# A two-layer hybrid backbone on one core: five sixths of the modulation vectors by GpSimd products and ScalarE row sums in place of TensorE matmuls

## The chip, the cores and the metric

One core of one Trainium2 chip runs the kernel. The time is device microseconds of one execution. TensorE (PE in the rows) multiplies, VectorE (DVE), ScalarE (ACT) and GpSimd (POOL) do the elementwise work, SyncE (SP) issues most of the DMAs. The outputs have to be the reference's to fp32 tolerances.

## What is computed

Two layers over 512 latent tokens and 256 context tokens, 1024 features, fp32. Each layer mixes the tokens in four ways (S5, Hyena long convolution, retention, latent attention) between one input and one output projection, and follows with a gated ConvFFN. Six vectors of 1024 numbers modulate each layer (the shifts, scales and gates of two norms), once from `c` for the latent tokens and once from `c_ctx` for the context:

```python
sc_lat = jax.nn.silu(c)
sc_ctx = jax.nn.silu(c_ctx)
for l in range(DEPTH):
    need_ctx = l < DEPTH - 1
    mod = sc_lat @ ada_w[l] + ada_b[l]
    sh1, sc1, g1, sh2, sc2, g2 = [m[:, None, :] for m in jnp.split(mod, 6, axis=-1)]
    modc = sc_ctx @ ada_w[l] + ada_b[l]
    ...
    h = modulate(rmsnorm(x, norm_g[l, 0]), sh1, sc1)
    y, yc = token_mixing(h, hc, w_in[l], w_out[l], s5_p, hy_p, ret_p, mla_p, need_ctx)
    x = x + g1 * rmsnorm(y, norm_g[l, 1])
    h = modulate(rmsnorm(x, norm_g[l, 2]), sh2, sc2)
    x = x + g2 * rmsnorm(conv_ffn(h, *ffn_p), norm_g[l, 3])
```

So 2 x 6144 columns of `ada_w` are multiplied by two vectors. The modulation is a product of a matrix with a vector or two: 24 MB of weights per layer are read for little arithmetic. In layer 1 the context's shift, scale and gate of the second half are needed by nobody, since the context leaves after layer 0's ConvFFN and layer 1's mixers.

## The kernel before

Features lie on partitions, tokens along the free dimension. Tokens are handled in pieces of 256 (one of the context, two of the latent stream); segment 0 is the context, segment 1 the latent stream. A product of two fp32 matrices is made in three passes of split operands: a weight tile of 128x1024 is loaded (tile `wr`, three buffers), ScalarE casts it to its high part (`wh`, L300), VectorE subtracts that for the low part (`wl`, L301), and TensorE multiplies high by high, high by low and low by high (`dense`, L336). All weight loads, activations, spills and tables go through SP's queue in program order; only a few small DMAs of the S5 and attention chains are issued by GpSimd (`qp`: L946, L947, L1336, L1338). Each engine works through its instructions in one order, which the tile framework's scheduler sets from the program order and priorities.

The modulation vectors come by thirds: `ada(l, b)` makes 2048 columns of layer `l`. It issues 16 loads of 512 KB (L470, tile `ar`, three buffers, which the Hyena chain's tables share), multiplies each with the two silu vectors on TensorE as stationary operand (L475, 64 matmuls a third, 128x32 by 128x512), copies the sum from PSUM (L478), transposes it by four matmuls (L481), and adds the bias. Six thirds: (0,0) at the start; (0,1) and (0,2) by `more`, one piece for each round of `ahead`; (1,0) as a filler of the `drain` that ends layer 0's output projection; (1,1) and (1,2) as a filler of the `drain` that ends layer 0's ConvFFN, and from there in layer 1's `ahead`.

The stages in order: start (norms, (0,0), tables); layer 0's input projection and mixers, woven by `ahead` (a round of every chain that is open for each step of the projection); the output projection, whose last tokens are finished by `live` chains (`finish`: row sum by TensorE, `n_row` by ScalarE L1440, scaling on VectorE, residual addition L1502 on GpSimd and VectorE by halves, squares L1504, modulated tiles H L1467); the ConvFFN (`run(g, W_FF)` at each weight load advances `prep1`, the preparation of layer 1: 62 calls); its last down products with `finish`; then layer 1 likewise. The attention chain (`mla`) splits queries and moves parts of them by DMA on GpSimd's queue (`B_Q`, `B_R`: L1336; `wh`, `wl` from `B_kr`: L1338) before its scores (L1325).

Of the kernel before, what the change touches and what calls it, by code (L numbers as in the profile page):

```python
# [19 lines left out]
L = 2  # L20
D = 1024
# [27 lines left out]
# ---------------------------------------------------------------- host layout  # L49
# [96 lines left out]
def _layout(inp):  # L146
# [5 lines left out]
    o["ada_w"] = _c(inp["ada_w"].reshape(L, KD, 128, 3, 2, 1024).transpose(0, 3, 1, 4, 2, 5))  # L152
# [68 lines left out]
# ---------------------------------------------------------------- the kernel  # L221
@with_exitstack
def tile_kernel(ctx, tc, I, out, dbg=None, upto=None):
# [15 lines left out]
    def tap(name, ap, a, b, k=None):  # L239
        """debug: columns a:b of a tensor (rows k of its tiles)"""  # L240
        if dbg is not None and name in dbg:
            d = dbg[name] if k is None else dbg[name][:, k]
            sp.dma_start(d[..., a:b], ap)
# [45 lines left out]
    # token ranges: segment 0 is the context, segment 1 the latent stream  # L289
# [3 lines left out]
    # ------------------------------------------------------------ helpers  # L293
# [17 lines left out]
    def blk(w, n=128):  # L311
        """tiles k of a loaded weight"""
        return lambda k: (w[0][:, k * n:(k + 1) * n], w[1][:, k * n:(k + 1) * n])

    def passes(W, ks):
        """stationary operand, which part of the moving one (0 high, 1 low), first, last"""
# [7 lines left out]
    def dense(W, X, ks, segs, fine=False, outs=None):  # L324
        """sum over k of W(k)^T X(k, seg, part), per segment into one PSUM bank"""
# [13 lines left out]
    class Job:  # L339
        """a dense product whose parts (256 tokens) may come one by one"""  # L340
# [18 lines left out]
    def ctx_room():  # L359
        """where two jobs share a bank for their context parts"""  # L360
# [11 lines left out]
    def open_jobs(keys, srcs, H, segs):  # L372
        """jobs of the next phase that run while the last tokens of this one are finished"""
# [34 lines left out]
    def rs_rows(p, items, chunks, w=1):  # L408
        """1/rms of columns of 128 tokens: items are ([K, tokens], [K, w]) pairs that add up"""
# [19 lines left out]
    # ------------------------------------------------------------ scratch in DRAM  # L429
# [16 lines left out]
    # ------------------------------------------------------------ adaLN vectors  # L446
# [5 lines left out]
    def ada_setup():  # L452
# [4 lines left out]
        act.activation(c2[:, :, 0:2], craw, AF.Silu)  # L457
        return c2
# [3 lines left out]
    def ada(l, b):  # L462
        """a third of the modulation vectors: 2048 columns"""
        md, der = mods[l]
        ps = sm_ps()
        for k in range(KD):
            raws = []
            for h in range(2):
                raw = new(wp, [128, 1024], "ar", bufs=3)
                qa.dma_start(raw, I["ada_w"][l, b, k, h])  # L470
# [11 lines left out]
        for r in range(2):  # L482
            v = md[:, 16 * b:16 * b + 16, r].rearrange("p (j i) -> p i j", i=4)
            s = pt.rearrange("p (i j x) -> p i j x", i=4, x=32)[:, :, :, r]
            dve.tensor_tensor(v, s, adab[:, l, 16 * b:16 * b + 16].rearrange("p (j i) -> p i j", i=4), ALU.add)
        gb = lambda i: ng[:, l, i].unsqueeze(2).to_broadcast([128, KD, 2])
# [4 lines left out]
        else:  # L491
            dve.scalar_tensor_tensor(der[:, 2], md[:, 32:40], 1.0, gb(2), ALU.add, ALU.mult)
            dve.tensor_tensor(der[:, 3], md[:, 40:48], gb(3), ALU.mult)
        yield

    # ------------------------------------------------------------ S5 parameters
    def reduce_turns(p, lam, n, tag):
        """re*dt, the reduced angle im*dt in turns, from [128, 3, n]"""
# [16 lines left out]
    def sincos(ang, k, out_):  # L515
        """ang[:, 0] holds turns; out_: [128, 2, n], the sine and the cosine"""
# [5 lines left out]
    def s5_prep(l, p):  # L522
# [25 lines left out]
        # a^1: power 1 sits at m = 6 (forward) and m = 1 (backward)  # L548
# [26 lines left out]
        for h in range(2):  # L575
            for d in (1, 0):
# [19 lines left out]
                # state inputs: transposed powers  # L596
# [7 lines left out]
                # state outputs  # L604
# [6 lines left out]
                # within-chunk kernels of two channel groups at a time; each other's are not used  # L611
# [26 lines left out]
        # rotations over chunks  # L638
# [24 lines left out]
    # ------------------------------------------------------------ hyena spectra  # L663
    def planes(al, z, R, room=None):
        """input planes of the classes of frequencies, class by class; z: [128, R/2, 256]; al: room by name"""
# [33 lines left out]
    def hy_spectra(l, p, n, nmx, dst):  # L699
# [33 lines left out]
        for o in range(2):  # L733
# [20 lines left out]
            # columns lie as (direction, channel)  # L754
# [813 lines left out]
    for l in range(L):  # L1568
# [47 lines left out]
        with ExitStack() as base, ExitStack() as esl, ExitStack() as esr:  # L1616
# [5 lines left out]
            if l == 0:  # L1622
# [9 lines left out]
                with mkpool("start", side="right") as px:  # L1632
                    g0 = ada(0, 0)
                    X = []
                    for i, (s, h) in enumerate(subs):
# [4 lines left out]
                        if i == 0:  # L1640
                            c2 = ada_setup()
# [338 lines left out]
```

## Time and profile before

| | |
|---|---|
| runs | 2124.91, 2129.36, 2129.20 us; median 2129.2 |
| profiled execution | span 2130.8 us |
| TensorE busy | 1992.2 us, 93% |
| VectorE, ScalarE, GpSimd busy | 1292.8 (61%), 781.8 (37%), 165.7 us (8%) |
| modulation matmuls (L475) | 384 records, 108.6 us |
| chain of waits | TensorE 77%, VectorE 8%, DMA 7% |

Busy times are sums over the span; stages differ, so a stretch is read by itself. In the tables of stretches each engine's busy time is followed by its instruction count in brackets, then the clock that TensorE was granted (a share of full speed), the busy share of the 16 DMA engines and GB/s. In timelines and the chain a row begins with start and length in us; what stands in square brackets is the engine's idle time before it and what ended it.

### The profile page before, as it was taken

To read this page: it belongs to the slowest core of one execution; us is meant where nothing else is said; L and a number is where in the kernel's file an instruction comes from. 1 tells how busy PE (TensorE), PEld (TensorE's weight loads), DVE (VectorE), ACT (ScalarE), POOL (GpSimd) and SP (SyncE) were. 2 spreads that over 40 slices of the span, in tenths; PEclk is the share of its full clock that TensorE was granted. 3 is DMA by queue.
4 is the path that set the end of the run, shared out by engine and by line. 5 is a ranking of instruction groups with operands and counts; after the bars stand their busy time and mean duration, and the time that the engine had idled before them with its cause. 6 is when DMAs were issued, how large, how long until landed. Compare 5 with 4: busy or idle time off the path is not lost.

```text
span 2130.8 us, 29370 instructions
## 1 busy us (share of the span) xinstructions
PE 1992.2 (93%) x11282; PEld 1558.7 (73%) x11282; DVE 1292.8 (61%) x2594; ACT 781.8 (37%) x1248; POOL 165.7 (8%) x180
## 2 busy tenths in 40 slices
PE   5899999889799999999999999899989989999997
PEld 1676775566687788788888886577766768888885
DVE  5767474786655876674645446367667356555555
ACT  3646322225144534433323234322243435333332
POOL 0121002211001020000000001100013110000000
PEclk7899999889999999999999999999989989999998
DMA  7566556634455434132422215877721314333331
GB/s 254 175 211 225 164 184 185 141 93 125 143 173 167 142 104 138 58 100 66 143 79 60 60 50 175 227 222 234 238 72 51 113 66 148 93 96 99 99 98 41
DMA packets 147092, 282.93 MB, mean 133 GB/s; under 512 B 35605, under 2 KB 78774, under 8 KB 146952
## 3 DMA queue, kind: packets, MB, share of 16 engines
q1 hardware_dynamic: 139016, 272.60, 40.7%
q0 software_dynamic: 3328, 7.13, 1.9%
q10 hardware_dynamic: 4608, 1.31, 0.3%
q8 instruction: 89, 1.46, 0.3%
q14 instruction: 51, 0.42, 0.1%
HBM read 229.07 MB, written 48.99 MB: 130 GB/s over the span
## 4 chain that ended last, share of the span: by engine, by line
PE 77%; DVE 8%; DMA 7%; issue 4%; ACT 2%; POOL 1%; SPq 1%; ACTq 0%; POOLq 0%; DVEq 0%
PE mm L336 44%; PE mm L1830 4%; PE sm L475 4%; DMA ar<-in_ada_w 3%; PE mm L351 2%; PE mm L1938 2%; PE sm L1434 2%; PE mm L1325 1%; PE sm L1380 1%; PE mm L1326 1%; PE mm L332 1%; PE mm L1327 1%; DMA wr<-in_w_v 1%; PE sm L745 1%; PE sm L845 1%
## 5 line engine op out<-in xcount | busy, mean ns | idle before, releaser
L301 DVE TENSOR_TENSOR wl<-wr,wh 128x1024 fp32r<-128x1024 f32 x174 | 212.9, 1225 | 313.8 <-ACT wh L300 309.6
L336 PE MATMUL mm<-H1h,wh 128*128 128x512 f32 x888 | 355.7, 401 | 4.1 <-ACT wh L300 4.0
L336 PE MATMUL mm<-H1h,wl 128*128 128x512 f32 x888 | 355.4, 400 | 0.8 <-DVE wl L301 0.8
L336 PE MATMUL mm<-H1l,wh 128*128 128x512 f32 x888 | 353.2, 398 | 0.0
L300 ACT CAST wh<-wr 128x1024 fp32r<-128x1024 f32 x174 | 182.3, 1050 | 369.2 <-PE mm L336 309.9
L336 PEld LDWEIGHTS mm<-H1h,wh 128*128 128x128 f32 x888 | 169.0, 190 | 52.8 <-ACT wh L300 9.5
L336 PEld LDWEIGHTS mm<-H1l,wh 128*128 128x128 f32 x888 | 168.9, 190 | 42.5 <-issue 5.6
L336 PEld LDWEIGHTS mm<-H1h,wl 128*128 128x128 f32 x888 | 169.0, 190 | 42.3 <-issue 5.0
L336 PE MATMUL mm<-H0h,wh 128*128 128x256 f32 x480 | 136.7, 285 | 5.2 <-DVE st L427 4.2
L336 PE MATMUL mm<-H0l,wh 128*128 128x256 f32 x480 | 138.0, 287 | 0.0
L336 PE MATMUL mm<-H0h,wl 128*128 128x256 f32 x480 | 137.8, 287 | 0.0
L336 PE MATMUL mm<-ff_mh,wh 128*128 128x512 f32 (+1 forms) x432 | 131.1, 357 | 1.0 <-DVE st L427 1.0
L336 PE MATMUL mm<-ff_mh,wl 128*128 128x512 f32 (+1 forms) x432 | 131.3, 357 | 0.0
L336 PE MATMUL mm<-ff_ml,wh 128*128 128x512 f32 (+1 forms) x432 | 130.3, 355 | 0.0
L475 PE MATMUL sm<-ar,ada_c 128*32 128x512 f32 x384 | 108.6, 687 | 16.1 <-DMA ar<-in_ada_w 16.1
L1502 POOL TENSOR_TENSOR x<-x,y 128x512 f32<-128x512 f32 x20 | 28.4, 1427 | 1105.0 <-DVE y L1501 873.1
L1888 DVE TENSOR_TENSOR y<-mm,y 128x512 f32<-128x512 f32 x80 | 53.5, 688 | 81.1 <-PE mm L336 80.9
L336 PEld LDWEIGHTS mm<-H0h,wh 128*128 128x128 f32 x480 | 92.0, 192 | 13.1 <-issue 9.5
L336 PEld LDWEIGHTS mm<-H0h,wl 128*128 128x128 f32 x480 | 91.6, 191 | 7.0 <-issue 6.9
L336 PEld LDWEIGHTS mm<-H0l,wh 128*128 128x128 f32 x480 | 91.5, 191 | 5.6 <-issue 5.3
L425 ACT ACTIVATE st<-mm,c_ffn_v 128x512 f32<-128x512 f32 (+1 forms) x132 | 88.7, 701 | 5.3 <-PE mm L351 5.3
L426 DVE SCALAR_TENSOR_TENSOR st<-mm,c_ffn_v,st 128x511 f32<-128x511 f32 (+1 forms) x132 | 83.0, 654 | 3.7 <-ACT st L425 3.7
(617 smaller groups left out, 4178.0 us busy)
## 6 DMA issues: line engine op xcount, KB each, us to landing
ar<-in_ada_w SPq DMA_DIRECT2D x96, 512.0 KB, 4.3
wr<-in_w_up SPq DMA_DIRECT2D x88, 512.0 KB, 3.6
wr<-in_w_down SPq DMA_DIRECT2D x44, 512.0 KB, 3.6
wr<-in_w_in SPq DMA_DIRECT2D x34, 512.0 KB, 4.8
wr<-in_w_out SPq DMA_DIRECT2D x16, 512.0 KB, 4.4
ar<-in_k_tabl SPq DMA_DIRECT2D x16, 512.0 KB, 3.7
xs_d<-x SPq DMA_DIRECT2D x8, 1024.0 KB, 5.6
pd<-st SPq DMA_DIRECT2D x19, 384.0 KB, 2.7
```

Of the source, the lines that this page charges most:

```text
L300: act.copy(hi, raw)
L301: dve.tensor_tensor(lo, raw, hi.bitcast(F32), ALU.subtract)
L336: pe.matmul(outs[s], w, X(k, s, j), start=f, stop=z)
L351: pe.matmul(self.outs[s][:, h:h + 256], w, X(k, s, j)[:, h:h + 256], start=f, stop=z)
L425: act.activation(u[:, o:o + m], ps, AF.Identity, bias=vw[:, 3:4], scale=vw[:, 1:2])
L426: dve.scalar_tensor_tensor(u[:, o + 1:o + m], ps[:, 0:m - 1], vw[:, 0:1], u[:, o + 1:o + m], ALU.mult, ALU.add)
L475: pe.matmul(ps[q:q + 32], c2[:, k], raws[h][:, j * 512:(j + 1) * 512], start=(k == 0), stop=(k == KD - 1))
L1434: pe.matmul(self.ps[q:q + 32, :256], ones32, sq[:, i], start=(self.k < 4), stop=(self.k >= KD - 4))
L1502: (pool, dve)[k // 2 % 2].tensor_tensor(x[:, ks], x[:, ks], y[:, ks], ALU.add)
L1830: pe.matmul(ps[:, m * 256:(m + 1) * 256], w, C[s][j][:, k, h:h + 256], start=f and not e and m == 0, stop=z and m == 1)
L1888: dve.tensor_tensor(d, ps, d, ALU.add)
L1938: pe.matmul(ps[:, m * 256:(m + 1) * 256], w, mid[k][j][:, tk:tk + 256], start=f, stop=z)
```

## The change

The weights of five thirds are stored transposed: 128 output columns on partitions, 1024 inputs along them, one tile of 512 KB for 128 outputs. `silu(c)` and `silu(c_ctx)` are broadcast over partitions once (two DMAs, two ScalarE activations). For each tile GpSimd multiplies elementwise (L519), and ScalarE copies the product onto itself with a row sum into the modulation vector (L520). The context's product goes to a single buffer `ada_s`, the other overwrites the weights. There are 16 tiles a third; two products each for layer 0's two thirds and for (1,0), one each for (1,1) and (1,2), which leave the context's out: 128 products and 128 row sums, with 80 loads as before. The first third (`ada_first`) stays on TensorE. 320 of the 384 matmul records go, with 5 ScalarE copies and 20 transposes. By the code all of layer 1's thirds run in `prep1`; the two drains lose their filler. A smaller scratch for GpSimd's DMAs makes room for the new tiles.

```diff
     o["c"] = ...
-    o["ada_w"] = _c(inp["ada_w"].reshape(L, KD, 128, 3, 2, 1024).transpose(0, 3, 1, 4, 2, 5))
+    aw = inp["ada_w"]
+    o["ada_w"] = _c(aw[0, :, :2048].reshape(KD, 128, 2, 1024).transpose(0, 2, 1, 3))
+    o["ada_t0"] = _c(aw[0, :, 2048:].T.reshape(32, 128, D))
+    o["ada_t1"] = _c(aw[1].T.reshape(48, 128, D))
+    o["c_row"] = _c(np.stack([inp["c"][0], inp["c_ctx"]]))
...
         act.activation(c2[:, :, 0:2], craw, AF.Silu)
+        for v in range(2):
+            sp.dma_start(cb[v], I["c_row"][v:v + 1].to_broadcast([128, D]))
         return c2
...
+    cb = [new(con, [128, D], f"c_bc{v}") for v in range(2)]
+
+    def ada_first():
...
+    def ada(l, b):
+        md = mods[l][0]
+        nr = 2 if l == 0 or b == 0 else 1
+        for m in range(16 * b, 16 * b + 16):
+            w = new(wp, [128, D], "ar", bufs=3)
+            qa.dma_start(w, I["ada_t0"][m - 16] if l == 0 else I["ada_t1"][m])
+            for r in reversed(range(nr)):
+                t = new(con, [128, D], "ada_s") if r else w
+                pool.tensor_tensor(t, w, cb[r], ALU.mult)
+                act.activation(t, t, AF.Copy, accum_out=md[:, m, r:r + 1])
+            if m % 2:
+                yield
+        for r in range(nr):
+            v = md[:, 16 * b:16 * b + 16, r]
+            dve.tensor_tensor(v, v, adab[:, l, 16 * b:16 * b + 16], ALU.add)
+        ada_gains(l, b, nr)
         yield
...
-                    g0 = ada(0, 0)
+                    g0 = ada_first()
...
                             c2 = ada_setup()
+                    for v in range(2):
+                        act.activation(cb[v], cb[v], AF.Silu)
...
-                ga = ada(1, 0) if l == 0 else iter(())
-                drain(open_jobs([("up", i) for i in range(n)], [fl(I["w_up"][l, i]) for i in range(n)], H, lambda k: segs), ga)
+                drain(open_jobs([("up", i) for i in range(n)], [fl(I["w_up"][l, i]) for i in range(n)], H, lambda k: segs))
...
                 def prep1():
-                    yield from ga
+                    yield from ada(1, 0)
                     with mkpool("ps") as pq:
                         yield from s5_prep(1, pq)
                     with mkpool("ph") as pq:
                         yield from hy_spectra(1, pq, NL, "l", hy_K[1])
+                    yield from ada(1, 1)
+                    yield from ada(1, 2)
...
-                    if l < L - 1:
-                        ga = more(l + 1)
...
-                          if l < L - 1 else iter(()), ga)
+                          if l < L - 1 else iter(()))
+                    ga = None
...
-    nc = bacc.Bacc("TRN2", target_bir_lowering=False, num_devices=1)
+    nc = bacc.Bacc("TRN2", target_bir_lowering=False, num_devices=1, dynamic_dma_scratch_size=4096)
```

What follows is the order of the instructions on three engines at the places that matter, before and after. Lines of the changed kernel are 4 to 36 higher than before.

GpSimd in layer 0's mixers, before: the moves of the attention's operands (`wl` from `B_kr`; `B_Q` and `B_R`, its queries) and of S5's (`A_U`, `A_T`), with a copy between.

```order
L1338 DMA wl_3384<-B_kr_2938 33x768
L1338 DMA wl_3392<-B_kr_2938 33x768
L946 DMA A_U_3528<-s_u_25_102 16x16x128 x4
L1204 COPY A_SB_3185<-rq_y_3171 128x512
L946 DMA A_U_3528<-s_u_25_102 16x16x128
L947 DMA A_T_3529<-s_T_18_95 16x16x128 x2
L1336 DMA B_Q_3381<-st_3377 32x768
L1336 DMA B_R_3382<-st_3378 32x768
L1336 DMA B_Q_3389<-st_3377 32x768
L1336 DMA B_R_3390<-st_3378 32x768
```

The moves of the queries stand next to each other here.

GpSimd at the same place after the change; `ar` and `ada_s` are the modulation products.

```order
L979 DMA A_U_3614<-s_u_25_102 16x16x128
L519 TENSOR_TENSOR ada_s_3220<-ar_3218,c_bc_90_167 128x1024
L1369 DMA B_Q_3474<-st_3470 32x768
L519 TENSOR_TENSOR ar_3218<-ar_3218,c_bc_89_166 128x1024
L519 TENSOR_TENSOR ada_s_3334<-ar_3332,c_bc_90_167 128x1024
L1369 DMA B_R_3475<-st_3471 32x768
L519 TENSOR_TENSOR ar_3332<-ar_3332,c_bc_89_166 128x1024
L1237 COPY A_SB_3266<-rq_y_3252 128x512
L519 TENSOR_TENSOR ada_s_3341<-ar_3339,c_bc_90_167 128x1024
L1369 DMA B_Q_3482<-st_3470 32x768
L519 TENSOR_TENSOR ar_3339<-ar_3339,c_bc_89_166 128x1024
```

A move for the attention now has two or three products of 128x1024 ahead of it.

ScalarE at the end of layer 0's output projection, before: the row of the last 256 tokens (`n_row`), their squares (L1504, `x` is the residual) and modulated tiles (`H0h`), with ConvFFN evictions (L425) between.

```order
L1440 COPY n_row_5861<-sm_5531 128x256
L1504 ACTIVATE y_5529<-x_5527 128x512 x3
L425 ACTIVATE st_6159<-mm_5811,c_ffn_v_88 128x512
L1504 ACTIVATE y_5529<-x_5527 128x512
L425 ACTIVATE st_6200<-mm_5818,c_ffn_v_88 128x512
L1440 COPY n_row_6034<-sm_5948 128x256
L425 ACTIVATE st_6273<-mm_5825,c_ffn_v_88 128x512
L1467 ACTIVATE H0h_5803<-y_5529,mod_85_162 128x256 x6
```

Only two evictions lie between the row and the tiles.

ScalarE at the same place after; `ada_s` and `ar` are the modulation's row sums.

```order
L1473 COPY n_row_5938<-sm_5617 128x256
L520 ACTIVATE ada_s_6550,mod_87_164<-ada_s_6550 128x1024
L520 ACTIVATE ar_6548,mod_87_164<-ar_6548 128x1024
L520 ACTIVATE ada_s_6620,mod_87_164<-ada_s_6620 128x1024
L520 ACTIVATE ar_6618,mod_87_164<-ar_6618 128x1024
L520 ACTIVATE ada_s_6627,mod_87_164<-ada_s_6627 128x1024
L520 ACTIVATE ar_6625,mod_87_164<-ar_6625 128x1024
L1537 ACTIVATE y_5615<-x_5613 128x512 x3
L429 ACTIVATE st_6194<-mm_5897,c_ffn_v_88 128x512
L1537 ACTIVATE y_5615<-x_5613 128x512
```

Six row sums of layer 1's first third, which the code puts into the ConvFFN, stand between the row and the squares (now L1537). On GpSimd all 32 products of this third are ahead of these tokens' additions, ten of them ahead of the first tokens'.

SP at the end of layer 0's ConvFFN, before: saving residual tokens (`xs_d`) among modulation loads and the first weights of layer 1.

```order
L296 DMA wr_12052<-in_w_in 128x1024
L1930 DMA x_11085<-xs_d_90 128x8x256
L470 DMA ar_11394<-in_ada_w 128x1024
L470 DMA ar_11460<-in_ada_w 128x1024
L1951 DMA xs_d_90<-x_10917 1024x1x256
L470 DMA ar_11462<-in_ada_w 128x1024
L470 DMA ar_11540<-in_ada_w 128x1024
L470 DMA ar_11542<-in_ada_w 128x1024
```

The modulation loads (`ar`) go on like this down to the next weight tile of layer 1.

SP at the same place after the change:

```order
L300 DMA wr_12072<-in_w_in 128x1024
L300 DMA wr_12144<-in_w_in 128x1024
L300 DMA wr_12219<-in_w_in 128x1024
L1966 DMA x_11344<-xs_d_90 128x8x256
L1987 DMA xs_d_90<-x_11176 1024x1x256
L1987 DMA xs_d_90<-x_11344 1024x1x256
L300 DMA wr_12298<-in_w_in 128x1024
```

No modulation load is left here; all 32 stand among the ConvFFN's weight loads.

## Rows read from the trace of the kernel before

**Rows 1.** The page: the span, and the busy time of each engine
```profile
span 2130.8 us, 29370 instructions
PE 1992.2 (93%) x11282; PEld 1558.7 (73%) x11282; DVE 1292.8 (61%) x2594; ACT 781.8 (37%) x1248; POOL 165.7 (8%) x180
```

**Rows 2.** Busy time by stage (stretch, its us, each engine's busy us and count, clock, DMA)
```profile
0.00:62.00 62.00, 38.32 (x142) 10.39 (x143) 32.28 (x125) 24.94 (x38) 5.58 (x6) 0.71 0.79 259
62.00:280.00 218.00, 203.88 (x1186) 158.53 (x1184) 151.94 (x314) 111.24 (x191) 23.49 (x16) 0.97 0.57 185
280.00:370.00 90.00, 89.65 (x540) 57.33 (x538) 46.21 (x153) 21.06 (x46) 15.43 (x20) 0.96 0.64 196
...
600.00:705.00 105.00, 101.53 (x780) 80.13 (x779) 56.17 (x153) 42.32 (x87) 8.93 (x6) 1.00 0.51 167
705.00:1054.00 349.00, 346.12 (x1978) 292.62 (x1978) 236.43 (x427) 150.97 (x212) 20.02 (x12) 1.00 0.32 100
...
1255.00:1350.00 95.00, 89.05 (x611) 62.36 (x610) 55.99 (x167) 33.55 (x62) 7.74 (x6) 0.96 0.45 148
1350.00:1540.00 190.00, 176.37 (x1016) 138.18 (x1015) 113.37 (x231) 52.97 (x86) 10.19 (x26) 0.96 0.79 226
```

**Rows 3.** The same stretches, the matmuls of L475 alone
```profile
62.00:280.00 218.00, 15.80 (x64) 2.17 (x64) 0.97 0.57 185
280.00:370.00 90.00, 20.65 (x64) 2.65 (x64) 0.96 0.64 196
...
600.00:705.00 105.00, 12.28 (x64) 1.91 (x64) 1.00 0.51 167
...
1255.00:1350.00 95.00, 17.66 (x64) 2.70 (x64) 0.96 0.45 148
1350.00:1540.00 190.00, 17.46 (x64) 2.30 (x64) 0.96 0.79 226
```

**Rows 4.** Three groups by line: POOL's 128x1024 products, ACT's cast (ns min/median/max)
```profile
L607 POOL TENSOR_TENSOR q_tp<-q_trig,q_BC x8: 1922/1942/2854, 55.7 to 799.2; 128x1024 f32<-128x1024 f32 x8
...
L590 POOL TENSOR_TENSOR q_tp<-q_trig,q_bb x8: 1947/2786/3441, 51.0 to 795.1; 128x1024 f32<-128x1024 f32 x8
...
L300 ACT CAST wh<-wr x174: 1027/1052/1092, 12.3 to 2083.4; 128x1024 fp32r<-128x1024 f32 x174
```

**Rows 5.** Timeline 136 to 139 us, VectorE and POOL (start, us)
```profile
136.29 0.68 DVE L1086 TENSOR_TENSOR st<-st,r_rope 128x512 f32<-128x512 f32 x1
...
136.45 2.31 POOL L607 TENSOR_TENSOR q_tp<-q_trig,q_BC 128x1024 f32<-128x1024 f32 x1 [1.34 <-DVE q_PB L592]
...
136.89 2.42 DVE L1087 TENSOR_TENSOR st<-st,r_rope 128x512 f32<-128x512 f32 x1
```

**Rows 6.** Timeline 78 to 81 us, VectorE and POOL
```profile
78.29 0.16 DVE L1069 TENSOR_TENSOR g<-g,g 128x16 f32<-128x16 f32 x1
...
78.79 1.95 POOL L590 TENSOR_TENSOR q_tp<-q_trig,q_bb 128x1024 f32<-128x1024 f32 x1 [21.13 <-DVE g L1070]
78.85 1.92 DVE L1069 TENSOR_TENSOR g<-g,g 128x16 f32<-128x16 f32 x1
```

**Rows 7.** Timeline of POOL, 325 to 392 us
```profile
374.13 0.52 POOL L1336 DMA_DIRECT2D B_Q<-st  x1 [5.90 <-ACT st L392]
```

**Rows 8.** Timelines of ACT, end of the output projection and of the ConvFFN
```profile
680.30 0.63 ACT L1504 ACTIVATE y<-x 128x512 f32<-128x512 f32 x1 [11.02 <-POOL x L1502]
...
1343.01 1.31 ACT L1467 ACTIVATE H0h<-y,mod 128x256 fp32r<-128x256 f32 x3 [7.72 <-DVE y L1466]
```

**Rows 9.** Chain of waits, layer 1's in-projection
```profile
1378.16 18.18 DMA wr<-in_w_v
...
1443.80 5.15 DMA ar<-in_ada_w
...
1469.58 6.58 DMA ar<-in_ada_w
...
1489.93 4.09 DMA ar<-in_ada_w
```

More of the change, by code (lines that the diff above doesn't have):

```diff
@@ L457, in ada_setup @@
         act.activation(c2[:, :, 0:2], craw, AF.Silu)
+        for v in range(2):
+            sp.dma_start(cb[v], I["c_row"][v:v + 1].to_broadcast([128, D]))
         return c2
     mods = [(new(con, [128, 48, 2], f"mod{l}"), new(con, [128, 4, KD, 2], f"der{l}")) for l in range(L)]
-    def ada(l, b):
-        md, der = mods[l]
+    cb = [new(con, [128, D], f"c_bc{v}") for v in range(2)]
+    def ada_first():
+        md, der = mods[0]
         ps = sm_ps()
@@ L469, in ada @@
                 raw = new(wp, [128, 1024], "ar", bufs=3)
-                qa.dma_start(raw, I["ada_w"][l, b, k, h])
+                qa.dma_start(raw, I["ada_w"][k, h])
                 raws.append(raw)
@@ L482, in ada, with ada_gains @@
         for r in range(2):
-            v = md[:, 16 * b:16 * b + 16, r].rearrange("p (j i) -> p i j", i=4)
+            v = md[:, 0:16, r].rearrange("p (j i) -> p i j", i=4)
             s = pt.rearrange("p (i j x) -> p i j x", i=4, x=32)[:, :, :, r]
-            dve.tensor_tensor(v, s, adab[:, l, 16 * b:16 * b + 16].rearrange("p (j i) -> p i j", i=4), ALU.add)
-        gb = lambda i: ng[:, l, i].unsqueeze(2).to_broadcast([128, KD, 2])
+            dve.tensor_tensor(v, s, adab[:, 0, 0:16].rearrange("p (j i) -> p i j", i=4), ALU.add)
+        ada_gains(0, 0, 2)
+        yield
+    def ada_gains(l, b, nr):
+        md, der = mods[l]
+        md, der = md[:, :, :nr], der[:, :, :, :nr]
+        gb = lambda i: ng[:, l, i].unsqueeze(2).to_broadcast([128, KD, nr])
         if b == 0:
@@ L493, in ada @@
             dve.tensor_tensor(der[:, 3], md[:, 40:48], gb(3), ALU.mult)
+    def ada(l, b):
[9 more added lines that the diff above has]
+            if m % 2:
+                yield
+        for r in range(nr):
+            v = md[:, 16 * b:16 * b + 16, r]
+            dve.tensor_tensor(v, v, adab[:, l, 16 * b:16 * b + 16], ALU.add)
+        ada_gains(l, b, nr)
         yield
```

## Prediction

> **What bounds the kernel now.** I read the page first, for the busy times [rows 1]: TensorE works 1992 of 2131 us, GpSimd 8% of them. The execution behind the profile spans 2130.8 us, 1.6 more than the median of the three runs (2129.2). All sums below are made against 2130.8, and 1.6 is taken off at the end. A difference of 0.2%, 4.3 us, is about what a measurement of this kernel can tell from none.
>
> Next comes busy time by stage [rows 2], since a share of the whole span says little about any stage. The stretches are: 0 to 62 us the start; 62 to 370 layer 0's projections and mixers; 600 to 705 the last mixer products and the output projection; 705 to 1054 most of the ConvFFN; 1255 to 1350 its last products and the end of the layer; 1350 to 1540 layer 1's in-projection. See that TensorE fills 99% of the ConvFFN, but 93% of layer 1's in-projection, and that VectorE has 152 of 218 us in 62 to 280, so it is far from idle where the change puts most of its GpSimd work.
>
> Then the modulation matmuls alone [rows 3]. Five thirds leave TensorE: 15.80 + 20.65 + 12.28 + 17.66 + 17.46 = 83.85 us. That is the ceiling, and it falls due only where TensorE is what the stage waits for.
>
> **What one product costs.** The trace has GpSimd products of 128x1024 [rows 4]: medians of 1.94 us at one line and 2.79 at the other, the longest 3.44. I take the middle of the medians, 2.36 us, and keep 1.94 and 3.44 as ends. The row sum on ScalarE is not there as such; the 128x1024 cast at 1.05 us is nearest, so 1.05, with half and double of it, 0.5 and 2.1, as ends. With 32 in a 90 us stretch beside 21 us of other ScalarE work [rows 2], 1.05 makes 55 of 90 and even 2.1 no more than 88.
>
> VectorE pays too. In one stretch [rows 5] a 128x512 product took 0.68 us, and the next of the same shape 2.42 while a GpSimd product ran: 1.74 more. In another [rows 6] a 128x16 product of 0.16 us became 1.92, and ended with the GpSimd product it met. So one GpSimd product can hold one VectorE operation for its own length; I charge 0.87 us per product, the middle of no delay and 1.74.
>
> **Start: +4 us.** Two vectors are broadcast to 128 partitions, 1.05 MB more; at the stage's 259 GB/s [rows 2] that is 4 us, and two Silu of about 1.05 us lie beside it. Ends 0 and +6. The first third stays as it is.
>
> **62 to 280 us: −5.** 15.80 us of matmuls go, 32 products come. GpSimd: 23.5 + 32 × 2.36 = 99 of 218 us, not the bound. VectorE: 152 + 32 × 0.87 = 180 of 218, fuller but not full. Its operations split weights and evict products, so TensorE waits for them oftener. I take a third of 15.8. Ends: −15.8, and +19, if a third of 32 delays of 1.74 us lay on the path.
>
> **280 to 370 us: +1.** Here 20.65 us of matmuls go, and half of the layer's 64 products come, as half of the matmuls do now. GpSimd becomes the fullest engine: 15.4 + 32 × 2.36 = 91 us for a stretch of 90. What stands behind the products matters: attention's queries are moved by DMAs that GpSimd issues (in the order above next to each other before the change, with two products between one and the next after it). Today such a DMA waits for nothing on its queue, only for ScalarE's part of the query [rows 7]. Attention cannot begin before all of them and the last products are through. Ends: 15.4 + 32 × 1.94 = 77, so −13; 15.4 + 32 × 3.44 = 125, so +35. I take the +1 of 2.36, between the medians; 2.79 would make it 105 us, +15.
>
> **600 to 705 us: +3.** By its code layer 1's first third runs in the ConvFFN; in the order it stands here, its 32 products ahead of the last residual additions on GpSimd, and six row sums ahead of ScalarE's last squares. Ten products are through before the first addition, so the row of them can begin by 600: 32 × 2.36 = 76 us plus 8.9 of GpSimd's own gives 684. Those squares start at 680 now after waiting 11.02 us for the GpSimd addition [rows 8]: +4. Of the 12.28 us of matmuls that leave, 11 lay inside that wait: −1. Ends: −12, and +18 (at 2.79: 698).
>
> **705 to 1255 us: 0.** The other 32 products of layer 1 come here, under a TensorE at 346 of 349 us. VectorE has 236 of 349, and 32 × 0.87 = 28 more. Loads are 0.5 MB at a time on a DMA system at 0.32 [rows 2]. What hides them is TensorE; if VectorE's splits came late, the end would be +5.
>
> **1255 to 1350 us: −10.** 17.66 us of matmuls go. But the stage ends with a chain: ScalarE's last modulated tiles wait 7.72 us for VectorE [rows 8], while TensorE had those matmuls to fill. 17.66 − 7.72 = 9.9. Ends −17.7 and 0.
>
> **1350 to 1540 us: −18.** 17.46 us of matmuls go from a TensorE that is busy 176 of 190. The loads that SP issues among layer 1's weights go as well. The chain of waits shows three waits for such loads, 5.15, 6.58 and 4.09 us, and one of 18.18 for a weight tile [rows 9], which can stay: the DMA engines are busy for 79% of this stage, with much else. I take the matmul time alone. Ends: −31 (with all of TensorE's idle 13.6 us), and 0 if weights and evictions are what it waits for.
>
> **Sum.** 4 − 5 + 1 + 3 + 0 − 10 − 18 = −25: 2105.8 for the profiled execution, **2104** against the median.
>
> **Rivals.** (1) TensorE binds everywhere, the products hide: 2130.8 − 83.85 + 4, that is 2049 against the median. For it: TensorE's 93%. Against it: 91 us of GpSimd work for 90 us, and the chains at both stage ends. Chance 0.12.
>
> (2) On the other side: GpSimd's queue holds attention back. If its products take the 3.44 us that the longest took, 280 to 370 becomes 125 us, +35 in place of +1: 2130.8 − 25 + 34 = 2140, **2138** against the median. It decides from the length at which the loss eats up the other terms' −26: (90 + 26 − 15.4) / 32 = 3.1 us a product. For it: GpSimd's median beside a busy VectorE is already 2.79, ScalarE's row sums free its buffers and stand in a queue with evictions, and a single buffer holds the products of the context's row. Against it: the other line's median is 1.94. Chance 0.18.
>
> (3) VectorE binds. If every product kept VectorE out for its whole 1.94 us, then 64 × 1.94 = 124 on 151.9 + 46.2 = 198 makes 322 us for the 308 of 62 to 370: +14 where I have −4, so 2123.8, 2122 against the median. For it: the 1.92 us row [rows 6]. Against it: the other row's delay was 1.74 beside a GpSimd product of 2.31, and the 2.79 of GpSimd's slower line says that in part it is GpSimd which waits. [...] Chance 0.10.
>
> (4) The change does not do what it says: the matmuls only filled gaps. Then 1255 to 1350 and 1350 to 1540 give 0, and 2130.8 + 3 makes 2132 against the median. Layer 1's first third not landing in the ConvFFN is already in the sum. For it: TensorE is the chain's filler in both stages. Against it: 176 of 190. Chance 0.08.
>
> **How the numbers follow.** The forecast has 0.52, its own range 2088 to 2120. Faster: 0.52 + 0.12 + 0.06 of rival 3 = 0.70. Same: 0.04 of rival 3, 0.05 of rival 4, 0.02 of rival 2 = 0.11. Slower: 0.16 + 0.03 = 0.19. The range leaves out rival 1 and a third of rival 2, together 0.18: from 2062, where half of the ceiling's remainder would be had, to 2143, with rival 2 and a few microseconds more at the output projection.
>
> **What would show it.** Right: GpSimd busy near 165.7 + 128 × 2.36 = 468 us, TensorE down by 84, VectorE up by 70 to 110; attention's first scores within 15 us of where they stand; layer 1's in-projection shorter by 10 to 27. Wrong: products over 3.1 us, or attention's DMAs waiting for products for 20 us and more (rival 2); VectorE over 95% in 62 to 370 (rival 3); TensorE idle in 1255 to 1540 by what it lost in work (rival 4).

## The result and the profile after

The changed kernel takes 2239.2 us (four runs, 2236.64 to 2240.17) against 2127.5 for the kernel before, run beside it: a ratio of 1.0527, 95% interval 1.051 to 1.0544. It is 5% slower, where 2104 us, and at most 2143, had been forecast. The profiled execution spans 2236.7 us.

The page of the changed kernel, its span, busy times and the two groups of GpSimd's products:

```profile
span 2236.7 us, 29140 instructions
PE 1952.3 (87%) x10942; PEld 1581.1 (71%) x10942; DVE 1424.4 (64%) x2592; ACT 916.9 (41%) x1498; POOL 493.0 (22%) x308
...
L519 POOL TENSOR_TENSOR ar<-ar,c_bc 128x1024 f32<-128x1024 f32 x80 | 206.3, 2590 | 234.2 <-DMA ar<-in_ada_t 224.6
...
L519 POOL TENSOR_TENSOR ada_s<-ar,c_bc 128x1024 f32<-128x1024 f32 x48 | 117.5, 2448 | 243.1 <-DMA ar<-in_ada_t 214.6
```

Beside [rows 1]: TensorE works 40 us less, not 84. GpSimd's 128 products take 2.59 and 2.45 us in the mean, 324 us together, and with its other work GpSimd is busy for 493 us: the forecast 2.36 us each and 468 us were near. VectorE is busy 131.6 us more, though it has the same instructions: 1.03 us per product, where 0.87 had been charged. By busy time GpSimd (22%) and VectorE (64%) are still far from full.

To see where it went, each stage is measured from the first instruction of one piece of work to the first of the next, which are the same pieces in every kernel: the first transpose of S5's preparation, the first product of retention's queries and keys (its scores), S5's first chunk product, the first product of the output projection, the first early product of the ConvFFN, the first of its last down products, layer 1's first output product. Before, these stretches look like this (columns as in [rows 2]; they begin at 61.7, 283.6, 590.9, 664.4 and 1247.5 us):

```profile
61.70:283.60 221.90, 207.78 (x1216) 161.66 (x1214) 154.82 (x325) 112.36 (x194) 23.49 (x16) 0.97 0.57 185
283.60:398.40 114.80, 107.65 (x597) 69.56 (x597) 63.42 (x196) 26.62 (x56) 24.09 (x38) 0.92 0.70 191
590.90:664.40 73.50, 72.41 (x565) 62.07 (x564) 40.76 (x105) 35.55 (x70) 5.95 (x4) 1.00 0.45 151
664.40:1247.50 583.10, 577.46 (x3350) 486.41 (x3349) 346.40 (x609) 216.34 (x306) 23.00 (x14) 1.00 0.33 101
1247.50:1664.50 417.00, 385.29 (x2241) 283.20 (x2239) 257.82 (x581) 143.97 (x255) 50.12 (x69) 0.94 0.53 157
```

After:

```profile
66.20:340.70 274.50, 211.43 (x1161) 173.30 (x1159) 201.34 (x325) 144.44 (x256) 106.11 (x48) 0.85 0.47 152
340.70:488.20 147.50, 99.07 (x514) 76.17 (x513) 90.24 (x196) 60.55 (x118) 102.71 (x70) 0.75 0.54 144
686.20:800.10 113.90, 83.00 (x565) 69.58 (x564) 74.89 (x110) 61.48 (x118) 66.91 (x30) 0.85 0.45 149
800.10:1398.50 598.40, 574.40 (x3281) 491.02 (x3281) 368.15 (x611) 257.48 (x380) 120.40 (x50) 0.98 0.36 116
1398.50:1772.40 373.90, 341.66 (x2105) 273.51 (x2103) 256.08 (x574) 141.98 (x252) 50.87 (x69) 0.95 0.45 130
```

The first takes 274.5 us in place of 221.9. TensorE idles 63 us of it, 14 before (its waits for VectorE alone add up to 46.5 us, 10.9 before), and where it works it is slower: granted 0.85 of its clock, not 0.97, it is busy 211 us although 16 us of matmuls went. The second takes 147.5 for 114.8, the output projection's end 113.9 for 73.5, the ConvFFN 598.4 for 583.1. Only the fifth is shorter, 373.9 us for 417.0.

| stage | before | after | difference | forecast |
|---|---|---|---|---|
| to S5's preparation (start) | 61.7 | 66.2 | +4.5 | +4 |
| to retention's scores | 221.9 | 274.5 | +52.6 | −5 |
| to S5's first chunk product | 114.8 | 147.6 | +32.8 | +1 |
| to the output projection | 192.5 | 197.9 | +5.4 | none |
| to the ConvFFN's first early product | 73.5 | 113.9 | +40.4 | +3 |
| to its last down products | 583.1 | 598.5 | +15.4 | 0 |
| to layer 1's output projection | 416.9 | 373.8 | −43.1 | −28 |
| to the end | 466.3 | 464.3 | −2.0 | none |

What a lost stretch looks like from VectorE is seen in the output projection's end. Before, a reciprocal root is twelve operations on two columns that take 2.3 us from the first to the last:

```profile
633.39 0.16 DVE L399 TENSOR_SCALAR rq_v<-sm 128x2 f32<-128x2 f32 x1 [7.36 <-PE sm L1444]
...
635.55 0.16 DVE L405 SCALAR_TENSOR_TENSOR rq_y<-rq_a,rq_y 128x2 f32<-128x2 f32 x1
```

In the changed kernel (timeline of VectorE at the same place, second piece of tokens):

```profile
741.98 0.16 DVE L403 TENSOR_SCALAR rq_v<-sm 128x2 f32<-128x2 f32 x1 [9.67 <-PE sm L1477]
742.18 0.85 DVE L404 TENSOR_SCALAR rq_y<-rq_v 128x2 int32<-128x2 int32 x1
743.06 0.17 DVE L405 TENSOR_SCALAR rq_y<-rq_y 128x2 f32<-128x2 f32 x1
743.26 2.25 DVE L407 TENSOR_TENSOR rq_a<-rq_y 128x2 f32<-128x2 f32 x1
745.55 2.28 DVE L408 SCALAR_TENSOR_TENSOR rq_a<-rq_a,rq_v 128x2 f32<-128x2 f32 x1
747.86 0.16 DVE L409 SCALAR_TENSOR_TENSOR rq_y<-rq_a,rq_y 128x2 f32<-128x2 f32 x1
748.06 2.20 DVE L407 TENSOR_TENSOR rq_a<-rq_y 128x2 f32<-128x2 f32 x1
...
757.32 0.16 DVE L409 SCALAR_TENSOR_TENSOR rq_y<-rq_a,rq_y 128x2 f32<-128x2 f32 x1
```

and GpSimd in the same microseconds:

```profile
743.08 2.42 POOL L519 TENSOR_TENSOR ar<-ar,c_bc 128x1024 f32<-128x1024 f32 x1
745.44 2.37 POOL L519 TENSOR_TENSOR ada_s<-ar,c_bc 128x1024 f32<-128x1024 f32 x1
747.89 2.35 POOL L519 TENSOR_TENSOR ar<-ar,c_bc 128x1024 f32<-128x1024 f32 x1
750.20 2.34 POOL L519 TENSOR_TENSOR ada_s<-ar,c_bc 128x1024 f32<-128x1024 f32 x1
```

The first operation, which reads PSUM, takes 0.16 us. Each of those that read SBUF twice takes 0.16 us or, when a product is running, until that product ends: 743.26 to 745.51, 745.55 to 747.83, 748.06 to 750.26. So does the one at 742.18, which has a single operand in SBUF: it ends at 743.03, with the product before those shown. Where a product ends, one or two get through. The twelve take 15.5 us, and TensorE sits idle for most of that, waiting to broadcast the root:

```profile
757.63 0.66 PE L424 MATMUL sm<-c_k_ident,rq_y 128*128 128x128 f32 x2 [12.70 <-DVE rq_y L409]
```

It is so in the whole trace. Take the VectorE operations that start while a product still has 0.3 us or more to run, and call one held if it takes over 0.3 us longer than the shortest of its form. Of 63 with two operands in SBUF, 59 are held; of 15 `TENSOR_SCALAR` with their one operand in SBUF, 14; of 97 with an operand in PSUM, none.

### The profile page after: what moved, and what is told of

The parts are those of the page before. It is cut to its first block, busy times and chain, and to the rows that moved or that the text cites. A ratio compares the mean times of both kernels' runs of the same rounds, so it can differ in the third digit from the quotient of the medians.

```text
span 2236.7 us, 29140 instructions
## 1 busy us (share of the span) xinstructions
PE 1952.3 (87%) x10942; PEld 1581.1 (71%) x10942; DVE 1424.4 (64%) x2592; ACT 916.9 (41%) x1498; POOL 493.0 (22%) x308
## 5 line engine op out<-in xcount | busy, mean ns | idle before, releaser
L305 DVE TENSOR_TENSOR wl<-wr,wh 128x1024 fp32r<-128x1024 f32 x174 | 224.0, 1289 | 324.9 <-ACT wh L304 318.8
L519 POOL TENSOR_TENSOR ar<-ar,c_bc 128x1024 f32<-128x1024 f32 x80 | 206.3, 2590 | 234.2 <-DMA ar<-in_ada_t 224.6
L519 POOL TENSOR_TENSOR ada_s<-ar,c_bc 128x1024 f32<-128x1024 f32 x48 | 117.5, 2448 | 243.1 <-DMA ar<-in_ada_t 214.6
L520 ACT ACTIVATE ar<-ar 128x1024 f32<-128x1024 f32 x80 | 84.6, 1057 | 81.7 <-POOL ar L519 81.6
L340 PEld LDWEIGHTS mm<-H0h,wh 128*128 128x128 f32 x480 | 93.6, 195 | 18.7 <-issue 17.7
```

Source lines behind the costliest of these rows:

```text
L305: dve.tensor_tensor(lo, raw, hi.bitcast(F32), ALU.subtract)
L340: pe.matmul(outs[s], w, X(k, s, j), start=f, stop=z)
L519: pool.tensor_tensor(t, w, cb[r], ALU.mult)
L520: act.activation(t, t, AF.Copy, accum_out=md[:, m, r:r + 1])
```

## The experiments

Three theories. **Lock**: a GpSimd product keeps VectorE's operations on SBUF out while it runs. **Row sums**: ScalarE waits in its queue for products, and what stands behind (evictions, casts) is late. **Queue**: SyncE waits for buffers that a row sum has yet to read, and weight loads stand behind. All three have waits in the trace: in the stretch before retention's scores ScalarE waits 29 us for products in all, SyncE 23 us for row sums. Of the runs below, all but e11 are one execution each. Single executions of the kernel before lay between 2119.0 and 2140.6 us, so a difference of 20 us or less between two totals is not read as an effect; the stages are compared instead.

**e1: the products on VectorE.**

```diff
-                pool.tensor_tensor(t, w, cb[r], ALU.mult)
+                dve.tensor_tensor(t, w, cb[r], ALU.mult)
```

> The changed kernel (2239 us against 2127.5 before) with its 128 products on VectorE instead of GpSimd; loads, buffers and ScalarE's row sums stay. Theory L (lock: a GpSimd product of 2.4 us holds up each VectorE operation with two SBUF inputs that meets it, and chains of small ones meet one after another): the 128 products now take 1.23 us each of VectorE, about what they delayed it by, but no short chain is cut up by them; 2120 to 2165 us, VectorE's reciprocal-root chains back to 2.3 to 6 us. Theory R (row sums: ScalarE waits in its queue for the products, and evictions behind it are late): the waits stay, a product comes 1.2 us sooner; 2200 to 2240. Theory Q (SyncE's queue: loads that wait for a buffer until a row sum has read it hold back what is behind them): buffers come free little sooner; 2200 to 2240.

2117.4 us, against 2122.8 for the kernel before, run beside it. The page of e1:

```profile
span 2115.6 us, 29113 instructions
PE 1914.4 (90%) x10942; PEld 1554.0 (73%) x10942; DVE 1437.7 (68%) x2720; ACT 916.3 (43%) x1498; POOL 171.3 (8%) x180
```

VectorE is as busy as in the changed kernel (1437.7 and 1424.4 us): a product on it costs 1.22 us, about what one on GpSimd delays it by. But 122 us are back. The end of the output projection takes 72.5 us again. The miss: the chains in layer 0's mixers still take up to 12 us, as VectorE now has products of its own between their operations. Against theories of row sums and queue: the 128 row sums, the buffers and SyncE's order of loads are all still there. But ScalarE's waits for products are shorter too (70 us in the four stretches that lost time, 131 in the changed kernel), so e1 alone does not exclude the row sums; e9 does.

**e2: products and row sums of 128 columns**; **e3: whole products, row sums of 128 columns.** Both leave out seven eighths of the row sums of five thirds; the edit is e2's, e3 has its second change alone.

```diff
-                pool.tensor_tensor(t, w, cb[r], ALU.mult)
-                act.activation(t, t, AF.Copy, accum_out=md[:, m, r:r + 1])
+                pool.tensor_tensor(t[:, :128], w[:, :128], cb[r][:, :128], ALU.mult)
+                act.activation(t[:, :128], t[:, :128], AF.Copy, accum_out=md[:, m, r:r + 1])
```

> The changed kernel with products and row sums over the first 128 of 1024 columns only (seven eighths of the modulation's sums are left out): same instructions, loads, buffers and waits, GpSimd 0.3 and ScalarE 0.2 us each. It bounds what the durations cost. Theories L and R: nearly all of the loss goes, 2050 to 2110. Theory Q: the buffers are freed 6 us sooner each, so a part goes, but loads of 3.7 us and their order stay: 2110 to 2190.

> The changed kernel with whole products, but row sums over the first 128 of 1024 columns (the rest of the sums is left out): ScalarE's 128 row sums go from 1.06 to about 0.2 us, 110 us of ScalarE's time; its waits for GpSimd stay. Theory L: 2215 to 2240, since GpSimd's products stay. Theory R, if it is the length of the row sums: 2130 to 2200; if it is the wait for the product, 2215 to 2240 as well. Theory Q: about 1 us sooner for each buffer, 2200 to 2235.

2094.6 and 2216.3 us. With both short (products of 0.46 us in the median, where 0.3 had been expected), 144 us go; with the row sums alone short (0.31 us, not 0.2, each), 23. So most of the cost hangs on the length of the products, and the loads, which e2 keeps, cost little. e3 alone cannot tell the lock from ScalarE's waits for the product; e1 and e9 can.

**e4: the loads issued by GpSimd.**

```diff
-QUEUES = "ssssassssp"
+QUEUES = "pssssasssp"
```

> The changed kernel with the 80 modulation loads of 512 KB issued by GpSimd instead of SyncE. Theory Q: no weight load stands behind a load that waits for its buffer; 2130 to 2190, and SyncE's waits for the row sums (102 us in three stretches) nearly go. Theories L and R: 2225 to 2260, GpSimd pays some 0.6 us for each issue.

2265.4 us, 26 slower than the changed kernel and 5 above the range given for lock and row sums. SyncE's waits of modulation loads for row sums (41.8 us in 62 to 440 us in the changed kernel) are gone; its waits for the splits of weights stay (26.8 us there, 29.5 in the changed kernel). So the total speaks against the queue. The test is not clean: the edit moves the first third's 16 loads too, and GpSimd pays about 0.6 us for each of the 96 issues (0.59 in the median of the 80 transposed loads): the stretch to retention's scores is 14 us shorter (260.7), the start 8 and the next stretch 16 us longer. What the queue is worth shows in e9.

**e5: layer 0 on TensorE; e6: the same, with layer 1's products on VectorE; e7: layer 1's on VectorE, layer 0's on GpSimd.** In e5 and e6 `ada_first`, renamed `ada_pe`, takes its third as argument and makes all three of layer 0 from untransposed weights:

```diff
-                yield from ada(l, b)
+                yield from ada_pe(b)
...
-                    g0 = ada_first()
+                    g0 = ada_pe(0)
```

e6 has e1's edit besides; e7 has that edit for layer 1 alone (`(pool if l == 0 else dve).tensor_tensor`) and leaves layer 0 as changed.

> The changed kernel with all of layer 0's thirds on TensorE as before; layer 1's stay on GpSimd and ScalarE. Lock theory: the start and layer 0's mixers are as before (output projection begins near 591 us, not 686); its end and the ConvFFN lose what they lost in the changed kernel (40 and 15 us), the rest gains 43: 2125 to 2150 us. If the loss of the output projection's end came from layer 0's late mixers instead, the 40 us go as well: 2085 to 2110.

> As e5, and layer 1's 64 products on VectorE. Lock theory: nothing is blocked; layer 0 as before, the output projection's end and the ConvFFN within 5 us of before, and 43 us gained after the ConvFFN: 2080 to 2095 us, faster than both kernels. If VectorE's own 80 us of products hold up the ConvFFN's splits: 2100 to 2130.

> The changed kernel with layer 1's products on VectorE and layer 0's 64 on GpSimd. Lock theory: layer 0 loses what it lost in the changed kernel (about 95 us to the start of the output projection), the rest is as in e1: 2165 to 2200 us. If the two parts' losses do not add, below 2150.

The kernel before took 2139.3 us beside them; e5 2153.3, e6 2100.9, e7 2184.5. e5 is 3 and e6 6 us above the expected range. The stages come out as if cut out of either kernel:

| stage | before | after | e5 | e6 | e7 |
|---|---|---|---|---|---|
| to retention's scores | 221.9 | 274.5 | 223.3 | 223.5 | 275.5 |
| to S5's first chunk product | 114.8 | 147.6 | 113.6 | 110.2 | 146.2 |
| end of the output projection | 73.5 | 113.9 | 111.0 | 72.0 | 72.6 |
| ConvFFN | 583.1 | 598.5 | 599.7 | 590.6 | 587.2 |
| to layer 1's output projection | 416.9 | 373.8 | 377.1 | 375.9 | 377.6 |

Wherever the products are on GpSimd, a stage of layer 0's mixers or the output projection's end is long; nothing is carried from one stage into the next. All variants gain the 40 us after the ConvFFN. e6's one execution is 1.8% below the kernel before beside it.

**e8: each product in four pieces.**

```diff
-                pool.tensor_tensor(t, w, cb[r], ALU.mult)
+                for i in range(0, D, 256):
+                    pool.tensor_tensor(t[:, i:i + 256], w[:, i:i + 256], cb[r][:, i:i + 256], ALU.mult)
```

> The changed kernel with each GpSimd product in four pieces of 256 columns: the same work and the same row sums, GpSimd a little busier. Lock theory: a VectorE operation that meets a piece waits for 0.6 us, not 2.4; the chains of small operations in the output projection's end fall from 15 to under 8 us, and the time to 2160 to 2215. If it is GpSimd's total work, or the row sums behind it, that holds things up: 2235 to 2260.

2261.7 us: slower, as the other theories had it. VectorE at the output projection's end:

```profile
747.44 0.16 DVE L403 TENSOR_SCALAR rq_v<-sm 128x2 f32<-128x2 f32 x1 [11.42 <-PE sm L1478]
747.63 21.14 DVE L404 TENSOR_SCALAR rq_y<-rq_v 128x2 int32<-128x2 int32 x1
768.80 0.17 DVE L405 TENSOR_SCALAR rq_y<-rq_y 128x2 f32<-128x2 f32 x1
```

GpSimd (each row is four pieces):

```profile
746.78 2.85 POOL L520 TENSOR_TENSOR ada_s<-ar,c_bc 128x256 f32<-128x256 f32 x4
749.56 2.81 POOL L520 TENSOR_TENSOR ar<-ar,c_bc 128x256 f32<-128x256 f32 x4
...
765.95 2.79 POOL L520 TENSOR_TENSOR ar<-ar,c_bc 128x256 f32<-128x256 f32 x4
```

One operation on two columns, 0.17 us long elsewhere, took 21.14 us. GpSimd ran pieces back to back until 768.7, and VectorE's operation ended then. That is the extreme. Counted as above, 144 of 149 operations on SBUF that start inside a piece are held: 139 of them for 0.6 us or less, as expected, and five for 3.9 to 21 us, through several pieces. In the changed kernel 73 of 78 are held, most for about 2 us. So shorter pieces hold more operations for a shorter time, and now and then one for much longer; VectorE's busy time hardly changes (1420.4 us, 1424.4 in the changed kernel). A product in four pieces also takes 2.8 us, not 2.4, and GpSimd is busy for 565.6 us. The expectation was wrong in that the held time would shrink with the pieces: the root shown took 23 us, not under 8. Why the total is 22 us above the changed kernel's was not separated; most of it lies in the ConvFFN (613.0 us, 598.5 in the changed kernel).

**e9: memsets in place of products.** Five thirds of the modulation are left out.

```diff
-                pool.tensor_tensor(t, w, cb[r], ALU.mult)
+                pool.tensor_tensor(t[:, :4], w[:, :4], cb[r][:, :4], ALU.mult)
+                for n in (D, D, D // 2):
+                    pool.memset(t[:, :n], 0.0)
```

> The changed kernel with each GpSimd product replaced by a product of four columns (so that it waits for the same load) and memsets of 2560 elements a partition, which write and read nothing: five thirds of the modulation are left out (zeros). GpSimd is held about as long (2.4 us a product), ScalarE waits as before. Theory L in the form that it is two readers of SBUF that exclude each other: VectorE goes on, chains back to 2 to 6 us, 2100 to 2150 us. If GpSimd's length itself is what holds ScalarE, the buffers and GpSimd's own queue up: 2200 to 2250, as the changed kernel.

2131.2 us (before: 2127.6). The page of e9, and its stretches from 64.5, 304.1, 625.8 and 704.1 us:

```profile
span 2129.4 us, 29567 instructions
PE 1915.5 (90%) x10942; PEld 1554.2 (73%) x10942; DVE 1319.2 (62%) x2592; ACT 916.8 (43%) x1500; POOL 503.0 (24%) x692
```

```profile
64.50:304.10 239.60, 209.20 (x1200) 172.44 (x1198) 169.75 (x332) 147.15 (x261) 112.88 (x144) 0.92 0.55 179
304.10:429.30 125.20, 78.16 (x476) 59.72 (x476) 69.32 (x185) 55.31 (x109) 94.91 (x151) 0.81 0.56 158
625.80:704.10 78.30, 73.48 (x565) 62.26 (x563) 42.31 (x105) 54.44 (x106) 56.44 (x84) 1.00 0.66 222
704.10:1290.80 586.70, 571.02 (x3282) 489.81 (x3281) 353.76 (x616) 263.23 (x393) 136.06 (x183) 0.98 0.39 120
```

This is the run that separates the theories. GpSimd is as busy as in the changed kernel (503 us, 493 there), ScalarE too (916.8, 916.9), loads and buffers are the same, the waits nearly (in these four stretches ScalarE waits 118 us for what GpSimd writes, 131 in the changed kernel, and SyncE 205 us for row sums, 185 there), and 108 us are gone. VectorE's busy time is back to 1319 us, 26 above before. What the memsets lack, by the code, is reading SBUF; the product of four columns that is left before them takes 0.20 us in the median. Counted as above, of 97 operations with two operands in SBUF that start inside a memset only one is held, for 0.4 us; of 17 `TENSOR_SCALAR` on SBUF 14 still are, for up to 2.9 us, which is part of the 26. Nor is it that a product became four instructions: e8 has four as well, and is slower. TensorE's waits for VectorE in the four stretches come to 49 us, 116 in the changed kernel and 16 before. In the second stretch 10 us stay lost (125.2 for 114.8): this much may be GpSimd's queue or the row sums, and e1, which has no product on GpSimd, loses 12 there as well.

**e10: layer 1's first third later in the code of e5; e11: the same of e6.**

```diff
-                    yield from ada(1, 0)
                     with mkpool("ps") as pq:
...
+                    yield from ada(1, 0)
                     yield from ada(1, 1)
```

> e5 (layer 0 on TensorE, layer 1 on GpSimd) with layer 1's first third after the preparation of S5 and Hyena in the code, so that the scheduler no longer puts it into the end of the output projection. If that stage's 38 us come from those 32 products there: the stage back to 73 to 80 us, the ConvFFN up by some 10, 2110 to 2130 us (e5: 2153). If they come from the missing filler: 2145 to 2160.

> e6 (layer 0 on TensorE, layer 1's products on VectorE, 2101 us) with layer 1's first third later, as in e10: VectorE and ScalarE are free for the end of the output projection and the ConvFFN's start; 2085 to 2100 us. If the missing filler sets that stage, 2095 to 2105.

e10: 2145.3 us. The end of the output projection is back to 73.8 us, with the filler gone all the same, so its 40 us were the 32 products there. But the ConvFFN grows to 641.6, which was not expected, and so the total lies 15 us above the range: all 64 products now fall between 1015 and 1207 us. In this stretch TensorE is busy for 150 of 192 us at a clock of 0.88, and all of its waits are for VectorE, 42 us; ScalarE waits 84 us for products (from the waits in 1015 to 1207 us; us in all, times, longest):

```profile
PE mm L339 <- DVE st L430: 25.8, 7, 6.9
ACT ar L519 <- POOL ar L518: 60.8, 39, 4.2
ACT ada_s L519 <- POOL ada_s L518: 23.6, 14, 4.0
```

A TensorE that was 99% busy does not hide that: it waits for VectorE, mostly for evictions. Whether VectorE is late here by the lock or because ScalarE's casts stand behind row sums that wait for products was not separated.

e11: 2091.8 us (six runs, 2086.6 to 2100.9) against 2127.6 (eleven), ratio 0.9834, interval 0.9802 to 0.9867. It is 1.7% below the kernel before, and below the changed one. Its page:

```profile
span 2087.0 us, 29218 instructions
PE 1938.3 (93%) x11078; PEld 1547.4 (74%) x11078; DVE 1364.5 (65%) x2656; ACT 848.5 (41%) x1372; POOL 167.6 (8%) x180
```

VectorE has 72 us more than before, no operation waits for GpSimd's products, the ConvFFN takes 580.5 us and layer 1's way to its output projection 373.3.

**e12: e5 with reciprocal roots that read PSUM.** `a`, `yp` and a copy of `v` lie in a PSUM tile; each step that gives `y`, but the last, is done twice, to PSUM and to SBUF.

```diff
-        dve.tensor_tensor(a, y, y, ALU.mult)
-        dve.scalar_tensor_tensor(y, a, 1.5, y, ALU.add, ALU.mult)
+        dve.tensor_tensor(a, yp, y, ALU.mult)
+        dve.scalar_tensor_tensor(yp, a, 1.5, y, ALU.add, ALU.mult)
```

> e5 with the reciprocal-root chains of VectorE rewritten so that each of their small operations reads at most one operand from SBUF and the other from PSUM (16 operations in place of 12). Lock theory: GpSimd's products no longer stop them; the chains at the end of the output projection 3 to 4 us, not 10 to 15, and that stage 111 us down to 80 to 95, so 2120 to 2142 (e5: 2153). If VectorE is held by something else: 2150 to 2160.

2157.8 us, above the range of the lock theory and within the other. The chains in the output projection's end are 3.0 us each beside GpSimd's products, where e5 has 4.4, 17.0, 2.3 and 10.7: reading one operand from PSUM does free them. But the stage falls only from 111.0 to 101.3 us, and the mixers lose that again (S5's first chunk product comes 11 us later than in e5; why was not tried). So these chains are a quarter of that stage's loss, not most; the residual additions, splits and scalings of VectorE that also read SBUF twice are the natural rest, but they were not taken out one by one.

## Why the prediction was wrong

**What held, and what was off in size.** The start (+4 forecast, +4.5). A product's length (2.36, and 2.4 in the median). GpSimd's busy time, nearly (468 forecast, 493). That layer 1's first third would land in the output projection. The term "1255 to 1350 us: −10": from the first of the last down products to the end of the layer's last modulated tile it takes 91.9 us in place of 102.8. The term "1350 to 1540 us: −18" was mis-sized: from there to layer 1's first output product it takes 282.0 us in place of 314.2, so −32. There TensorE's busy time fell by 28.7 us, of which 17.5 are the modulation matmuls, and its idle time by 3.5; its clock was 0.95 for 0.93. Only the matmuls had been counted. VectorE's busy time rose by 132 us, where 70 to 110 had been forecast.

**The step that failed** is the one under "What one product costs": "I charge 0.87 us per product", and then asking whether VectorE's sum stays below the stage's length ("180 of 218, fuller but not full"; "What hides them is TensorE"). The size of the delay was near over the whole span, 1.03 us, but in the stretch to retention's scores it was 46.5 us for 32 products, 1.45 each. What was wrong above all is to treat it as throughput. VectorE's operations are links between TensorE and ScalarE (roots for a broadcast, splits of weights, residual additions), so a delay is on the path without VectorE being full: 201 of 274 us in the first stretch, where TensorE's waits for VectorE rose from 10.9 to 46.5 us. The forecast had the path only as the far end of that term, "+19, if a third of 32 delays of 1.74 us lay on the path". The row of 0.16 us that became 1.92 [rows 6] showed it, and that row should have been asked how many such operations follow one another: three rounds of three in each root. Also, in that stretch, where TensorE idled 63 us and not 14, its granted clock fell from 0.97 to 0.85, and the matmuls that stayed took 211 us in place of 192; the forecast had no term for that.

**By terms.** "62 to 280 us: −5" was +52.6; with products on VectorE (e1) +13.5, with memsets (e9) +17.7. "600 to 705 us: +3" was +40.4; e10 and e1 show that it is the products on GpSimd there, not the filler's absence. "705 to 1255 us: 0" was +15.4, and +58 in e10 with all 64 there: TensorE did not hide it, though how much of this is the lock is not shown. "280 to 370 us: +1" was +32.8 to S5's first product. There the GpSimd queue that rival 2 spoke of does its part:

```profile
433.18 0.53 POOL L1369 DMA_DIRECT2D B_Q<-st  x1 [1.75 <-ACT st L396]
433.72 2.75 POOL L519 TENSOR_TENSOR ar<-ar,c_bc 128x1024 f32<-128x1024 f32 x1
436.44 2.34 POOL L519 TENSOR_TENSOR ada_s<-ar,c_bc 128x1024 f32<-128x1024 f32 x1
438.73 0.55 POOL L1369 DMA_DIRECT2D B_R<-st  x1
```

The queries' moves are issued 5.5 us apart, each behind two products. But it did not take a product of over 3.1 us, as rival 2 had it, and without the lock (e9) two thirds of this loss are gone.

**The rivals.** Rival 3 had the right mechanism at a wrong price: it let the lock count only where VectorE would be full, which gave 2122. In the traces 59 of 63 operations with two SBUF inputs are held beside products, and one of 97 beside memsets. Rival 1 had the products hidden: TensorE's busy time fell by 40 us, not 84, and the time rose. Rival 4 is excluded: without filler the stretch that holds its two stages is 43 us shorter.

**What stays open:** how the 10 to 18 us that e9 and e1 still lose in each of the first two stretches divide between row sums, queues, the operations that are still held and TensorE's lower clock (0.92 and 0.81 in e9, 0.92 and 0.73 in e1, 0.97 and 0.92 before); what makes VectorE late in e10's ConvFFN; and which operations other than the roots make up the loss of the output projection's end.

## What to carry to other kernels

Work on an idle GpSimd was not free beside VectorE: each product here made VectorE 1.03 us busier. Before moving elementwise work there, list VectorE's operations in that stage that have two operands in SBUF (59 of 63 were held here), and its `TENSOR_SCALAR` on SBUF (14 of 15), and ask which of them TensorE or ScalarE waits for; their delay is a sum along a chain (15.5 us for a root of 2.3), not a share of busy time. The same work on VectorE itself, in a stage with a full TensorE, was cheaper (e11, with layer 1's products alone, 1.7% below the kernel before). Where TensorE comes to wait, price the lower clock as well as the gap (in the first stretch 63 us idle, not 14; a clock of 0.85, not 0.97; and 19 us more for the matmuls that stayed).

## What the runs showed of the hardware that was not expected

Cutting GpSimd's work into pieces of 0.74 us did not lessen VectorE's delay (busy for 1420.4 us, 1424.4 beside whole products): 139 of the 144 held operations got in after 0.6 us or less, but one of 0.17 us waited 21.14 us through a run of some thirty pieces (e8). Beside whole products of 2.4 us, 72 of the 73 held operations got in when the product that they met ended. Memsets on GpSimd, which by the code read nothing, left VectorE's busy time 26 us above before, where products of the same length in all made it 132 (e9); beside them operations with two operands in SBUF went on (one of 97 held), but `TENSOR_SCALAR` on SBUF was still held (14 of 17). An operation with one operand in PSUM was not held (none of 97 beside the changed kernel's products; roots of 3.0 us, e12).
